# Who subtracts the weights: a hybrid encoder step in which some subtractions and additions go from GpSimd to VectorE

## The chip, the cores and the metric

The kernel runs on one core of a Trainium2 chip. A core has five engines that run side by side, each with its own in-order line of instructions: TensorE (matmuls, "PE" in the profile, its weight loads "PEld"), VectorE ("DVE"), ScalarE ("ACT"), GpSimd ("POOL") and SyncE ("SP"), which here only issues transfers. They meet at semaphores. SBUF is the on-chip memory that they share, PSUM holds the matmul results in banks. The metric is the device time of one execution in microseconds; three executions of the kernel before gave 2524.32, 2525.68 and 2528.39 us, median 2525.68 us.

## The reference, cut to what matters

One layer of a streaming encoder, in float32, for 512 prompt tokens and 8 x 16 sample tokens (640 tokens in all, model width 2048):

```python
xn = rmsnorm(x, norm_mix)
qa, ka, va, qb, kb, vb = split(xn @ w_in)       # 3 x 1024 columns for group A, 1024 + 128 + 128 for group B
oa = band_attend(qa, ka, va, bias)              # 16 heads, own chunk and 8 before
ob = band_attend(rope(qb), rope(kb), vb, sink)  # 16 query heads, 2 key heads, window 128
x = x + concat(rmsnorm(oa), rmsnorm(ob)) @ w_out
h = rmsnorm(x, norm_ffn)
x = x + (silu(h @ w_gate) * (h @ w_up)) @ w_down   # inner width 5632
y = rmsnorm(x, norm_final)
```

The keys and values of both groups are outputs too.

## The kernel before

Everything is held transposed, features on the 128 partitions and the 640 tokens along the free dimension, in two halves of 320. To keep float32 precision with fast matmuls, each operand is split in two parts, `hi` (rounded to the matmul's type) and `lo` (what is left), and each product is three matmuls, `mm3` (L235 to L237): hi by hi, hi by lo, lo by hi. `Net.split` makes the parts: ScalarE writes `hi` (L226), VectorE subtracts it from the source to get `lo` (L227). The third matmul of a set, L237, is the first that needs the weights' `lo`.

The large products are done as **quartets**, a Strassen-like scheme (Winograd's form): four weight blocks b11, b12, b21, b22 against two token halves need seven products p1 to p7 in place of eight. The function `quartet(k, load, lefts, before, after, part, eng)` does one: it loads the four blocks (k chunks of 128 rows by 128 columns each, so k times 128 numbers for a partition), forms the differences of weights, and for each of the seven products splits one block and runs 3 k matmuls. Its differences, in the order of the program:

```python
b12 = b12 - b22        # VectorE, L843
s6  = b11 - b12        # VectorE, L847
p1: split(b11)
b11 = b22 - s6         # on GpSimd here (L850); if eng is VectorE, behind p7 instead (L855)
p6: split(s6);  p7: split(b12)
b21 = b21 - s6         # on eng (L859), behind p2: split(b21)
p5: split(b11);  p4: split(b21);  p3: split(b22)
```

The default of `eng` is `nc.gpsimd`. The order of the products is p1, p6, p7, p2, p5, p4, p3. The four weight tiles are slots of the list "W", the split parts slots of the list "H": four of them, that is two hi-lo pairs, in group A's quartets, six in the feed-forward part. A split therefore waits until TensorE has read the pair two (or three) products back. The products land in PSUM banks ("dn" for p1, p5, p6, p3, two tiles of two banks each; "at" for the others) and VectorE adds them up in SBUF (L869).

The stages, with their place in the profiled span:

- Group B's projections by plain products, to about 277 us.
- **Group A's quartets**, about 270 to 520 us: the loop over `order` runs ten quartets with k = 8, two output tiles each (20 of the 24 tiles of group A's queries, keys and values). After each, `collect` has gathered the two results; VectorE multiplies them by the token norm (L1051) or by it and 1/8 (L1053), and they are stored. During the last quartet the operands of group B's output projection are made (`release`, L231).
- Group A's attention and the sample attention beside the output projections, to about 860 us.
- Gate and up projections by 44 quartets with k = 8, to about 1930 us.
- **The down projection** in 32 steps, `step(t)`, one quartet each over the input blocks `active(t)`: k is 6 in steps 8 to 23 and 5 in the others. The last eight steps, 24 to 31, finish two output tiles each. Behind each of steps 24 to 29, `add_square` squares the two finished tiles on ScalarE (L322) and adds them to the running sum `ssq` (L323), on GpSimd unless told otherwise. Steps 30 and 31 run in an early and a late part, and step 31 alone has `eng=nc.vector`. GpSimd's line also issues the transfers of the activations, `fetch` (L1161).
- The final norm and the stores, from about 2490 us.

The order of instructions on each engine comes from a scheduler that goes by the order of the program, by what its own estimate of time says is ready, and by extra edges that the kernel adds: slots are handed on in order, `keep_follow` holds the first difference (L843) of a step with k under 8 behind the last split before it.

Of the kernel before, what the change touches and what calls it, by code (L numbers as in the profile page):

```python
# [29 lines left out]
STEPS = 32  # L30
# [309 lines left out]
def build(nc, tc, io, pools):  # L340
    n = Net(nc, tc, io, pools)
# [468 lines left out]
    def quartet(k, load, lefts, before=None, after=None, part="all", eng=nc.gpsimd):  # L810

        def product(src, which, bank):
            own = n.get("H"), n.get("H")
            hl = [r(sh(x, k, P)) for x in own]
            at = n.emitted()
            n.split(sh(src, k, P), *hl)
            n.last_split = at, n.emitted()
            if before:
                before(which)
            for j in range(k):  # L820
                n.mm3(bank, (hl[0][:, j], hl[1][:, j]), lefts[j][which][1], j == 0, j == k - 1)
            n.put("H", *own)
            if after:
                after(which)
            return bank

        def get(i):
            t = n.get("W")
            dma(out=sh(t, k, P), in_=load(i))
            return t  # L830

        w = slice(0, k * P)
        sub = ALU.subtract
        if part == "late":
            b21, b22 = get(2), get(3)
            for name, src, which in (("p2", b21, 4), ("p3", b22, 6)):
                yield name, product(src, which, n.bank()[:, :HT])
                n.put("W", src)
            return
        x, y = n.banks(), n.banks()  # L840
        b12, b22, b11 = get(1), get(3), get(0)
        at = n.emitted()
        nc.vector.tensor_tensor(b12[:, w], b12[:, w], b22[:, w], sub)  # L843
        if k < 8:
            n.follow.append((n.last_split, (at, n.emitted())))
        s6 = n.get("W")
        nc.vector.tensor_tensor(s6[:, w], b11[:, w], b12[:, w], sub)  # L847
        yield "p1", product(b11, 0, x[:, 0])
        if eng is nc.gpsimd:
            eng.tensor_tensor(b11[:, w], b22[:, w], s6[:, w], sub)  # L850
        yield "p6", product(s6, 1, y[:, 0])
        yield "p7", product(b12, 2, n.bank()[:, :HT])
        n.put("W", b12)
        if eng is not nc.gpsimd:
            eng.tensor_tensor(b11[:, w], b22[:, w], s6[:, w], sub)  # L855
        b21 = get(2)
        if part == "all":
            yield "p2", product(b21, 4, n.bank()[:, :HT])
        eng.tensor_tensor(b21[:, w], b21[:, w], s6[:, w], sub)  # L859
        n.put("W", s6)  # L860
        yield "p5", product(b11, 3, x[:, 1])
        n.put("W", b11)
        yield "p4", product(b21, 5, n.bank()[:, :HT])
        n.put("W", b21)
        if part == "all":
            yield "p3", product(b22, 6, y[:, 1])
        n.put("W", b22)
# [3 lines left out]
    def collect(steps):  # L871

        y = []
        for name, bank in steps:
            if name == "p1":
                y.append(n.get("S"))
                c11, c21 = y[0][:, :HT], y[0][:, HT:]
                nc.scalar.activation(c11, bank, AF.Identity)
            elif name == "p6":
                y.append(n.get("S"))  # L880
                c12, c22 = y[1][:, :HT], y[1][:, HT:]
                add(c12, c11, bank)
            elif name == "p7":
                add(c21, c12, bank)
            elif name == "p5":
                add(c22, c21, bank)
                add(c12, c12, bank)
            elif name == "p2":
                add(c11, c11, bank)
            elif name == "p4":  # L890
                add(c21, c21, bank)
            elif name == "p3":
                add(c12, c12, bank)
            yield name, y
# [31 lines left out]
    sums = [[None] * 7 for _ in range(8)]  # L926
# [111 lines left out]
    for at in range(0, len(order), 2):  # L1038
        two = order[at:at + 2]
        ws = [io["w_in"][8 * i + p] for i, p in two]  # L1040
        load = lambda z: ws[z % 2][:, 8 * (z // 2):8 * (z // 2) + 8]
        last = at + 2 == len(order)
        if last:
            n.streams = (("heads 0", "heads"), ("decode 0", "decode"), ("heads 1", "heads"), ("decode 1", "decode"))
            for p in range(8):
                heads_of(prompt_a, p, [])
        for _, y in collect(quartet(8, load, sums, split_thirds if at == 0 else None, release if last else None)):
            pass
        for (i, p), x in zip(two, y):
            if i:  # L1050
                nc.vector.tensor_tensor(x, x, r_mix, ALU.mult)  # L1051
            else:
                nc.vector.scalar_tensor_tensor(x, x, 0.125, r_mix, ALU.mult, ALU.mult)  # L1053
            keep_a(i, p, x)
# [13 lines left out]
    r_a, ssq = n.get("S"), n.get("S")  # L1068
# [183 lines left out]
    for i in range(NPAIR):  # L1252
        for src in ("w_gate", "w_up"):
            blocks = [(2 * i, 0), (2 * i + 1, 0), (2 * i, 8), (2 * i + 1, 8)]
            load = lambda z: io[src][blocks[z][0], :, blocks[z][1]:blocks[z][1] + 8]
            y = [n.get("S")]
            c11, c21 = y[0][:, :HT], y[0][:, HT:]
            start, end = i == 0 and src == "w_gate", i == NPAIR - 1 and src == "w_up"
            for step, bank in quartet(8, load, hs, (lambda w: next(prep)) if start else None, free if end else None,
                                      eng=nc.vector if start else nc.gpsimd):  # L1260
# [64 lines left out]
    def step(t, part="all"):  # L1325
        now = active(t)
        nxt = active(t + 1) if t + 1 < STEPS else []
        cnt, q, last = len(now), t % 8, t >= STEPS - 8

        def after(which):  # L1330
            gone = [j for j in now if j not in nxt]
            n.put("S", *(lefts[j][which][0] for j in gone))
            if t == 0:
                fetch_late()
                if which in (0, 1, 2):
                    split_raws()
                    n.follow.append((border, n.later[-1]))
                if which in (2, 4, 3):
                    at = n.emitted()
                    next(final, None)  # L1340
                    n.later.append((at, n.emitted()))
                for x in {3: (0,), 5: (1, 2), 6: (4, 3, 5, 6)}.get(which, ()):
                    keep_last(x)
            waiting.append([(j, which) for j in nxt if j not in now and j != NPAIR - 1])
            fetch_waiting(2)

        if t < 8:
            x, y = n.get("S"), n.get("S")
            sums.append((x, y, n.get("S") if q % 2 == 0 else sums[-1][2]))
            if t == 0:  # L1350
                load_sums()
        x, y, u = sums[q]
        c11, c21, c12, c22 = x[:, :HT], x[:, HT:], y[:, :HT], y[:, HT:]
        us = u[:, HT * (q % 2):HT * (q % 2) + HT]
        o = 2 * sum(len(active(i)) for i in range(q, t, 8))

        def load(z):
            if z == 0 and 0 < t < 8:
                load_sums()
            return io["w_down"][q + 8 * (z % 2), :, o + cnt * (z // 2):o + cnt * (z // 2) + cnt]  # L1360

        for name, bank in quartet(cnt, load, [lefts[j] for j in now], None, after, part,
                                  nc.vector if t == STEPS - 1 else nc.gpsimd):
            if name == "p1":
                if t < 8:
                    nc.scalar.activation(us, bank, AF.Identity)
                else:
                    add(us, us, bank)
                add(c11, c11, bank)
            elif name == "p6":  # L1370
                add(us, us, bank)
            elif name == "p7":
                add(c21, c21, bank)
                add(c22, c22, bank)
            elif name == "p5":
                add(c22, c22, bank)
                add(c12, c12, bank)
            elif name == "p2":
                add(c11, c11, bank)
            elif name == "p4":  # L1380
                add(c21, c21, bank)
            elif name == "p3":
                add(c12, c12, bank)
            if last and name == ("p5" if part == "early" else "p2" if part == "all" else None):
                for c in (c21, c22, c12):
                    add(c, c, us)
            yield name
# [5 lines left out]
    for t in range(STEPS - 2):  # L1393
        run(t)
        if t >= STEPS - 8:
            if t == STEPS - 8:
                ssq = n.get("S")
            for i in range(2):
                n.add_square(ssq, sums[t % 8][i], t == STEPS - 8 and i == 0, "S")
            if t == STEPS - 8:  # L1400
                nc.scalar.activation(n.small(1), ssq[:, :1], AF.Sqrt)

# [141 lines left out]
```

## Time and profile before

| | |
|---|---|
| median of three executions | 2525.68 us |
| profiled execution, its time | 2525.74 us |
| profiled execution, its span | 2523.9 us |
| TensorE busy | 2480.9 us (98%) |
| VectorE busy | 1977.1 us (78%) |
| ScalarE busy | 1055.8 us (42%) |
| GpSimd busy | 697.3 us (28%) |
| GpSimd differences, L850 and L859 | 84 and 84, 182.3 and 186.3 us |
| GpSimd additions of squares, L323 | 29, 49.2 us |

A row of the groups of instructions reads: line, engine, operation, output from inputs, shape, count | busy time, mean ns of one | idle time before them and what ended it. A row of the timeline reads: start in us, length in us, engine, line, operation, and in brackets the idle time before it and what ended that. A row of a table by stage has the stage's bounds, its length, and for each engine its busy time with the number of instructions that ran in it. Matmuls overlap: each is shown some 0.31 us long but the next starts 0.147 us later, so a short pause of TensorE hardly shows in its busy time. The number of matmuls in a stretch shows it better.

### The profile page before, as it was taken

The numbers are of one execution on the slowest core, as the hardware profiler recorded it, in microseconds if no ns is written. First come the engines' busy times: TensorE is split into PE (matmuls) and PEld (weight loads), VectorE is DVE, ScalarE is ACT, GpSimd is POOL, SyncE is SP. The second block draws the span as 40 slices with busy tenths as digits, with TensorE's granted clock in tenths as the row PEclk, the third lists the DMA queues.
The fourth block names the chain that finished last, engine by engine and source line by source line (L and its number), as shares of the span: only waits on it lengthen the run. The fifth ranks groups of instructions, "written<-read, shape, count | busy, mean of one in ns | idle before, by whom it ended". The sixth has DMA issues, their size and how long they took to land.

```text
span 2523.9 us, 44564 instructions
## 1 busy us (share of the span) xinstructions
PE 2480.9 (98%) x17285; PEld 2415.7 (96%) x17285; DVE 1977.1 (78%) x2945; ACT 1055.8 (42%) x1701; POOL 697.3 (28%) x566
## 2 busy tenths in 40 slices
PE   9999999999999999999999999999999999999997
PEld 8888999987899999999999999999999999999997
DVE  7667776685658887788888888888889877777797
ACT  5446333265545543443444343334334333333342
POOL 1001211111002043333323233332325433333353
PEclk9999999999999999999999999999999999999998
DMA  5224433378664334543443344334437766666655
GB/s 198 92 91 122 166 134 124 133 251 289 224 211 155 133 116 146 175 137 122 134 143 128 129 134 144 121 127 143 136 129 260 216 187 181 170 176 177 175 158 182
DMA packets 191604, 401.68 MB, mean 159 GB/s; under 512 B 22496, under 2 KB 83936, under 8 KB 191392
## 3 DMA queue, kind: packets, MB, share of 16 engines
q1 hardware_dynamic: 164608, 340.51, 41.1%
q0 software_dynamic: 23184, 52.77, 7.6%
q10 hardware_dynamic: 3600, 5.55, 0.6%
q8 instruction: 136, 2.23, 0.4%
q14 instruction: 76, 0.62, 0.1%
HBM read 311.14 MB, written 86.87 MB: 158 GB/s over the span
## 4 chain that ended last, share of the span: by engine, by line
PE 87%; DVE 8%; DMA 2%; ACT 1%; issue 1%; POOL 0%; SPq 0%; DVEq 0%; ACTq 0%; POOLq 0%
PE dn L235 17%; PE dn L237 17%; PE dn L236 17%; PE at L237 10%; PE at L236 10%; PE at L235 10%; DVE W L227 2%; PE at L363 2%; PE at L489 1%; DVE S L869 1%; PE at L450 1%; DMA W<-w_in 1%; DMA S<-first_d 1%; ACT W L226 1%; PE at L785 0%
## 5 line engine op out<-in xcount | busy, mean ns | idle before, releaser
L226 ACT ACTIVATE W<-W 128x1024 fp32r<-128x1024 f32 (+2 forms) x662 | 640.3, 968 | 1058.1 <-PE dn L236 559.4
L235 PE MATMUL dn<-S,W 128*128 128x320 f32 x3374 | 1054.3, 313 | 4.2 <-ACT W L226 2.7
L237 PE MATMUL dn<-S,W 128*128 128x320 f32 x3374 | 1045.7, 310 | 7.3 <-DVE W L227 7.0
L236 PE MATMUL dn<-S,W 128*128 128x320 f32 x3374 | 1043.5, 309 | 0.3 <-DVE S L227 0.3
L227 DVE TENSOR_TENSOR W<-W,W 128x1024 fp32r<-128x1024 f32 (+2 forms) x662 | 798.4, 1206 | 93.1 <-ACT W L226 86.0
L235 PEld LDWEIGHTS dn<-S,W 128*128 128x128 f32 x3374 | 633.8, 188 | 19.5 <-issue 14.5
L237 PEld LDWEIGHTS dn<-S,W 128*128 128x128 f32 x3374 | 633.4, 188 | 13.1 <-DVE W L227 11.5
L236 PEld LDWEIGHTS dn<-S,W 128*128 128x128 f32 x3374 | 633.9, 188 | 1.2 <-DVE S L227 0.6
L237 PE MATMUL at<-S,W 128*128 128x320 f32 x1834 | 568.7, 310 | 4.2 <-DVE W L227 4.2
L235 PE MATMUL at<-S,W 128*128 128x320 f32 x1834 | 567.9, 310 | 0.5 <-ACT W L226 0.5
L236 PE MATMUL at<-S,W 128*128 128x320 f32 x1834 | 567.6, 309 | 0.0
L850 POOL TENSOR_TENSOR W<-W,W 128x1024 f32<-128x1024 f32 (+2 forms) x84 | 182.3, 2170 | 776.7 <-DVE W L227 598.2
L237 PEld LDWEIGHTS at<-S,W 128*128 128x128 f32 x1834 | 345.0, 188 | 6.0 <-DVE W L227 5.5
L235 PEld LDWEIGHTS at<-S,W 128*128 128x128 f32 x1834 | 345.1, 188 | 0.8 <-ACT W L226 0.8
L236 PEld LDWEIGHTS at<-S,W 128*128 128x128 f32 x1834 | 345.0, 188 | 0.0
L869 DVE TENSOR_TENSOR S<-S,dn 128x320 f32<-128x320 f32 x398 | 182.0, 480 | 76.0 <-PE dn L237 76.0
L859 POOL TENSOR_TENSOR W<-W,W 128x1024 f32<-128x1024 f32 (+2 forms) x84 | 186.3, 2218 | 185.0 <-DVE W L227 136.8
L869 DVE TENSOR_TENSOR S<-S,at 128x320 f32<-128x320 f32 x292 | 138.1, 482 | 95.6 <-PE at L237 93.5
L843 DVE TENSOR_TENSOR W<-W,W 128x1024 f32<-128x1024 f32 (+2 forms) x86 | 119.5, 1390 | 39.7 <-DMA W<-w_gate 28.1
L847 DVE TENSOR_TENSOR W<-W,W 128x1024 f32<-128x1024 f32 (+2 forms) x86 | 95.8, 1114 | 59.3 <-DMA W<-w_up 33.3
L1161 POOL DMA_DIRECT2D S<-act_d x161 | 87.9, 547 | 160.9 <-PE dn L237 79.6
L1225 DVE TENSOR_TENSOR S<-S,half 128x320 fp32r<-128x320 f32 x147 | 119.7, 835 | 2.9 <-ACT half L1223 1.0
(175 smaller groups left out, 1699.7 us busy)
## 6 DMA issues: line engine op xcount, KB each, us to landing
S<-act_d POOLq DMA_DIRECT2D x161, 320.0 KB, 3.7
W<-w_gate SPq DMA_DIRECT2D x88, 512.0 KB
W<-w_up SPq DMA_DIRECT2D x88, 512.0 KB
W<-w_in SPq DMA_DIRECT2D x66, 512.0 KB
W<-w_down SPq DMA_DIRECT2D x64, 384.0 KB
act_d<-half SPq DMA_DIRECT2D x147, 160.0 KB
act_d<-S SPq DMA_DIRECT2D x147, 160.0 KB
W<-w_down SPq DMA_DIRECT2D x68, 320.0 KB
```

Source lines behind the costliest of these rows:

```text
L226: self.nc.scalar.activation(hi, src, AF.Identity)
L227: self.nc.vector.tensor_tensor(lo, src, f(hi), ALU.subtract)
L235: mm(out, a[0], b[0], start=first, stop=False)
L236: mm(out, a[0], b[1], start=False, stop=False)
L237: mm(out, a[1], b[0], start=False, stop=last)
L843: nc.vector.tensor_tensor(b12[:, w], b12[:, w], b22[:, w], sub)
L847: nc.vector.tensor_tensor(s6[:, w], b11[:, w], b12[:, w], sub)
L850: eng.tensor_tensor(b11[:, w], b22[:, w], s6[:, w], sub)
L859: eng.tensor_tensor(b21[:, w], b21[:, w], s6[:, w], sub)
L869: add = lambda o, a, b: nc.vector.tensor_tensor(o, a, b, ALU.add)
L1161: nc.gpsimd.dma_start(out=r(sh(t, 2, HT)), in_=r(act_d[which, :, j]))
L1225: nc.vector.tensor_tensor(r(src), src, hi, ALU.subtract)
```

## The change

Three places get VectorE where they had GpSimd.

- The ten quartets of group A are called with `eng=nc.vector`. So both differences that GpSimd made there (L850, L859) are VectorE's, and the first of them (then L855) stands behind p7's split in the program, no longer in front of p6's.
- In the down projection `eng` is VectorE for all of the last eight steps, and not for the last alone: seven more steps.
- The additions of squares behind steps 24 to 29 (eleven, since the first square is written straight to `ssq`) go to VectorE; the squares themselves stay on ScalarE.

Nothing that is computed changes.

```diff
@@ group A's loop @@
-        for _, y in collect(quartet(8, load, sums, split_thirds if at == 0 else None, release if last else None)):
+        for _, y in collect(quartet(8, load, sums, split_thirds if at == 0 else None, release if last else None,
+                                    eng=nc.vector)):
             pass
@@ step(t) of the down projection @@
         for name, bank in quartet(cnt, load, [lefts[j] for j in now], None, after, part,
-                                  nc.vector if t == STEPS - 1 else nc.gpsimd):
+                                  nc.vector if t >= STEPS - 8 else nc.gpsimd):
@@ behind steps 24 to 29 @@
             for i in range(2):
-                n.add_square(ssq, sums[t % 8][i], t == STEPS - 8 and i == 0, "S")
+                n.add_square(ssq, sums[t % 8][i], t == STEPS - 8 and i == 0, "S", nc.vector)
```

## The prediction

> **What bounds the kernel now.** I read the busy shares first, then counted matmuls by stage in the stages that the change touches, and then looked in the timeline at what VectorE and GpSimd do at the places where the count falls short.
>
> ```profile
> span 2523.9 us, 44564 instructions
> PE 2480.9 (98%) x17285; PEld 2415.7 (96%) x17285; DVE 1977.1 (78%) x2945; ACT 1055.8 (42%) x1701; POOL 697.3 (28%) x566
> ```
>
> TensorE is the bound: outside its busy time there are 43 us. An edit on another engine can only win back pauses of TensorE in its own stage. Here are the stages (columns: bounds, length, busy time with count for PE, PEld, DVE, ACT, POOL, then clock and transfers):
>
> ```profile
> 1000.00:1900.00 900.00, 900.00 (x6138) 899.91 (x6137) 754.40 (x824) 356.08 (x455) 290.98 (x147) 1.00 0.41 135
> ...
> 270.00:282.00 12.00, 10.51 (x70) 10.02 (x69) 11.00 (x12) 2.77 (x4) 3.35 (x1) 1.00 0.55 187
> 282.00:470.00 188.00, 187.19 (x1268) 185.72 (x1267) 126.74 (x135) 58.51 (x60) 36.19 (x15) 1.00 0.37 129
> 470.00:482.00 12.00, 10.69 (x72) 10.16 (x71) 9.43 (x10) 3.50 (x4) 2.41 (x1) 1.00 0.38 131
> 482.00:510.00 28.00, 28.00 (x193) 28.00 (x192) 16.72 (x20) 10.04 (x11) 4.83 (x2) 1.00 0.48 158
> 510.00:520.00 10.00, 8.29 (x55) 7.77 (x54) 10.00 (x11) 8.14 (x12) 4.10 (x3) 1.00 0.83 278
> 2340.00:2420.00 80.00, 80.00 (x548) 80.00 (x547) 67.34 (x100) 31.75 (x43) 33.47 (x35) 1.00 0.62 176
> 2420.00:2476.00 56.00, 54.33 (x362) 52.89 (x362) 55.81 (x75) 25.38 (x38) 33.31 (x31) 1.00 0.60 171
> 2476.00:2490.00 14.00, 13.22 (x87) 12.42 (x86) 13.65 (x26) 4.92 (x8) 1.66 (x4) 1.00 0.62 189
> 2490.00:2524.00 34.00, 19.54 (x120) 19.01 (x118) 19.27 (x47) 6.55 (x15) 8.37 (x10) 0.70 0.45 155
> ```
>
> The first row is TensorE undisturbed: 900 us / 6136 = 0.1467 us for a matmul (two are always in flight, so each stretch counts two more than start in it). At that rate 12 us holds 84, 188 us 1283.5, 10 us 70, 56 us 384, 14 us 97.5. So TensorE loses 14 matmuls or **2.05 us** at the first quartet of group A, 15.5 or **2.3 us** over its next seven borders, 12 or **1.75 us** at one late border, 15 or **2.2 us** in its last quartet, nothing in between (193 of 193); in the down projection 22 or **3.2 us** from 2420 to 2476 and 10.5 or **1.5 us** to 2490, and nothing before 2420 although VectorE and GpSimd already meet there. That is 13.0 us, the most that this change can win. The last 34 us hold other work and stay.
>
> **What makes VectorE late.** In the last steps VectorE is busy all the time (55.81 of 56 us), yet not by its own work:
>
> ```profile
> 2418.71 2.08 DVE L227 TENSOR_TENSOR W<-W,W 128x640 fp32r<-128x640 f32 x1
> 2420.71 0.47 DVE L869 TENSOR_TENSOR S<-S,dn 128x320 f32<-128x320 f32 x1
> 2421.11 1.80 DVE L227 TENSOR_TENSOR W<-W,W 128x640 fp32r<-128x640 f32 x1
> ...
> 2447.87 0.81 DVE L843 TENSOR_TENSOR W<-W,W 128x640 f32<-128x640 f32 x1
> 2448.61 0.87 DVE L869 TENSOR_TENSOR S<-S,dn 128x320 f32<-128x320 f32 x2
> 2449.40 0.81 DVE L847 TENSOR_TENSOR W<-W,W 128x640 f32<-128x640 f32 x1
> ```
>
> ```profile
> 2418.53 1.57 POOL L850 TENSOR_TENSOR W<-W,W 128x640 f32<-128x640 f32 x1 [2.42 <-DVE W L227]
> 2420.65 1.57 POOL L323 TENSOR_TENSOR S<-S,S 128x640 f32<-128x640 f32 x1
> ```
>
> An operation of the split's size takes 0.81 us at 2447.87 and the split 2.08 or 1.80 us beside a GpSimd operation, while the addition from a PSUM bank (L869, 2420.71) keeps its 0.47 us beside one. So an operation of VectorE with both inputs in SBUF stands still while GpSimd runs one.
>
> The Trainium skill, page "SBUF — State Buffer", section "SBUF: two separate sides", says this of the port pair that the two engines share: it is locked for a whole instruction, the loser fully blocks, and a VectorE operation with at most one SBUF input does not contend. These rows agree, the PSUM addition included: the second split began 0.46 us into the 1.57 us of GpSimd's addition and came out 0.99 us long over, where the lock leaves 1.11. By the lock alone four operations could hold VectorE for 4 x 1.57 = 6.3 us a step and not the 4.4 us that I find below; the last steps would then return all of their 3.2 us, my sum being 2.6.
>
> **The change part by part: the last steps.** From the rows above, consecutive starts give VectorE 0.735 us for a 640-wide operation and 0.40 for a 320-wide addition. A step holds seven splits, two differences and 13 additions: 9 x 0.735 + 13 x 0.40 = 11.8 us. One step lasts 16.2 us and VectorE fills it, so 4.4 us of it is standing still for four GpSimd operations (two differences, two squares), 1.1 us each:
>
> ```profile
> 2418.53:2434.75 16.22, 15.90 (x108) 15.53 (x108) 16.18 (x23) 7.46 (x11) 8.94 (x10) 1.00 0.66 183
> ```
>
> After the change the four cost VectorE 4 x 0.735 = 2.9 us and the 4.4 us go: 14.75 us a step. TensorE needs 105 x 0.1467 = 15.4 us. So VectorE drops below TensorE, by 4%. The pauses end if the scheduler's order fits in that margin; the pairs of slots (three) let the splits run about two products, 4.4 us, ahead. Of the 3.2 us that TensorE loses there I take **2.6** (bounds 0 and 3.2; the case below 0 is a rival). From 2476 GpSimd is nearly idle already (1.66 us), and the 1.5 us there is backlog that VectorE brings along (13.65 of 14 us busy); with less of it about half comes back: **0.8** (0 to 1.5). GpSimd's transfers of activations in the same line come earlier, if anything.
>
> **Group A.** GpSimd's first difference lasts 2.4 us here (2413 ns in the mean of nine) and falls on the border between two quartets, where VectorE has a row of work with both inputs in SBUF:
>
> ```profile
> 347.57 0.83 DVE L1051 TENSOR_TENSOR S<-S,S 128x640 f32<-128x640 f32 x1
> 350.80 1.90 DVE L1051 TENSOR_TENSOR S<-S,S 128x640 f32<-128x640 f32 x1
> ...
> 472.45 1.23 DVE L843 TENSOR_TENSOR W<-W,W 128x1024 f32<-128x1024 f32 x1 [2.25 <-DMA W<-w_in]
> ...
> 476.50 2.73 DVE L1053 SCALAR_TENSOR_TENSOR S<-S,S 128x640 f32<-128x640 f32 x1
> ...
> 510.91 3.83 DVE L231 SCALAR_TENSOR_TENSOR S<-S,gains,S 128x640 fp32r<-128x640 f32 x2
> ```
>
> ```profile
> L1051 DVE TENSOR_TENSOR S<-S,S 128x640 f32<-128x640 f32 x12 | 16.9, 1411 | 0.4
> L1053 DVE SCALAR_TENSOR_TENSOR S<-S,S 128x640 f32<-128x640 f32 x6 | 9.7, 1622 | 0.2
> L850 POOL TENSOR_TENSOR W<-W,W 128x1024 f32<-128x1024 f32 x9 | 21.7, 2413 | 112.9 <-DVE W L227 112.9
> ```
>
> Eighteen of these, two at each of nine borders, cost 26.6 us where 18 x 0.83 = 14.9 would do: 1.3 us of standing still at each border, right ahead of the split of p6, for which L237 then waits. The moved difference costs VectorE 1.13 us (1024 wide, consecutive starts):
>
> ```profile
> 267.60 1.21 DVE L843 TENSOR_TENSOR W<-W,W 128x1024 f32<-128x1024 f32 x1
> 268.73 1.68 DVE L227 TENSOR_TENSOR S<-W,S 128x320 fp32r<-128x320 f32 x4
> ```
>
> If it stands in the same place, 0.2 us is won at each border; if it fits a gap, 1.3. The pauses are mostly 0.3 to 0.6 us, so a little is enough: of 2.3 us I take **1.6** (0 to 2.3). The other difference, L859, is made in the middle of a quartet, beside an idle VectorE:
>
> ```profile
> 332.53 1.06 ACT L226 ACTIVATE W<-W 128x1024 fp32r<-128x1024 f32 x1 [2.41 <-PE dn L236]
> 333.62 1.23 DVE L227 TENSOR_TENSOR W<-W,W 128x1024 fp32r<-128x1024 f32 x1 [0.41 <-ACT W L226]
> 336.19 0.49 DVE L869 TENSOR_TENSOR S<-S,at 128x320 f32<-128x320 f32 x1 [1.35 <-PE at L237]
> ```
>
> There it wins nothing and costs 1.13 us in gaps of 1.35 us; stage-wide VectorE has room (126.74 of 188 us, and 15 x 1.13 = 17 more). What it costs without that cover: a split ends at 334.85 and its third matmul comes at about 336.6 (its slots were free when ScalarE began the same split, 1.09 us ahead of VectorE at 332.53; one product of 24 x 0.1467 = 3.5 us and some matmuls follow), so 1.75 us of slack stands against 1.13. I take 0.
>
> First quartet: L843 took 2.88 us against 1.21 and the reading of a PSUM result queued behind it:
>
> ```profile
> 274.38 2.88 DVE L843 TENSOR_TENSOR W<-W,W 128x1024 f32<-128x1024 f32 x1 [0.48 <-DMA W<-w_in]
> 277.17 0.81 DVE L435 TENSOR_TENSOR S<-dn,S 128x640 f32<-128x640 f32 x1
> ```
>
> 1.67 us go, 1.13 may come in front: 0.54 at least, 2.05 at most, taken **1.2**. Late border: the stretched L1053 (2.73, so 1.9 over) explains the second of two pauses there, about 0.8 us; the first goes back to a late weight load (L843 sat idle 2.25 us for it) and stays. Taken **0.7** (0 to 0.8). Last quartet: the two L231 lose 3.83 - 1.68 = 2.15 us to L859 and would stand behind its 1.13 us instead: **1.0** (0 to 2.2).
>
> **The sum.** 1.2 + 1.6 + 0.7 + 1.0 + 2.6 + 0.8 = 7.9 us. The profiled execution took 2525.74 us (span 2523.9 and 1.8 around it), the median of three is 2525.68; so 2525.7 - 7.9 = **2517.8 us**. The lower ends together give 0.5 us, 2525; the upper ends 12.0, about 2513.7. What a measurement of this kernel can tell from no change is about 0.2%, 5 us, so faster begins below 2520.6.
>
> **The rivals.**
>
> *The stall changes its cause only.* The moved differences stand just where VectorE stood still (0.735 for 1.1, 1.13 for 1.3), in front of the same splits, and a 4% margin is not enough for an in-order line. For it: the program's order makes the difference ready at the same moment as now. Against: each swap is still a small gain. Half of my sum, 4 us: 2521.7, chance 0.27.
>
> *VectorE's line waits for the squares.* An addition of squares now stands in the line that makes every split, and waits there for ScalarE:
>
> ```profile
> 2418.82 0.74 ACT L322 ACTIVATE S<-S 128x640 f32<-128x640 f32 x1 [0.31 <-DVE S L869]
> 2421.22 0.74 ACT L322 ACTIVATE S<-S 128x640 f32<-128x640 f32 x1 [1.03 <-DVE S L869]
> 2407.76 0.74 ACT L226 ACTIVATE W<-W 128x640 fp32r<-128x640 f32 x1 [1.41 <-PE dn L236]
> ```
>
> If nothing is put in between, each costs 0.31 + 0.74 = 1.05 us, and 1.4 more if ScalarE sits on a split that waits for its slots (2407.76). Behind it queue all splits, and TensorE behind those. At 0.3 us a square the margin (15.4 - 14.75) is gone, at 0.73 the step is as long as now (16.2), at 1.1 the gain of group A is used up too (0.8 us a step over five and a half steps). At 1.8 us, between 1.05 and 2.45, a step is 18.35 us: 5.5 x 2.95 = 16.2 lost where 3.2 are now, 13 more, less 4.5 won in group A: 2534, **slower**. Against: VectorE's line has a whole product's work that can stand between a square and its addition. Chance 0.12.
>
> *All comes back,* also the 1.5 us at the end: 2513.7, chance 0.13.
>
> **How the numbers follow.** The forecast, 2515 to 2520.6 with a little above, has 0.48. Faster: 0.13 and 0.43 of the 0.48, 0.56. Same: 0.27 and the 0.05 that is left, with a little of the square case, 0.33. Slower: 0.11. The range takes the upper ends of the terms and part of the square case: 2513 to 2529, with about 0.1 left out on either side.
>
> **What would show it.** The splits of the last steps, today (2385 to 2473):
>
> ```profile
> L227 DVE TENSOR_TENSOR W<-W,W 128x640 fp32r<-128x640 f32 x39 | 49.1, 1259 | 1.3 <-ACT W L226 1.0
> ```
>
> Their mean falls from 1.26 us to 0.82; the step from 16.2 to 15.4 us; VectorE's busy share there from full to about 0.95; L1051 and L1053 to 0.83; 384 matmuls and not 362 in the 56 us before the last two steps. Wrong would be: idle time of VectorE ahead of L323 ended by ScalarE's L322, L237 still waiting for L227 at the borders, or a pause in the gate and up projections that isn't there now.

## The result, and the profile after

The changed kernel took 2513.18 us (median of five, 2512.12 to 2516.12) where the kernel before took 2525.68 us: 12.5 us less, a ratio of 0.9953 with a 95% interval of 0.9942 to 0.9963. That is faster beyond the 0.2% that can be told, inside the range, and 4.6 us below the forecast. It lies only 0.2 us above the range's lower end, 2513. The profiled execution has a span of 2511.4 us:

```profile
span 2511.4 us, 44507 instructions
PE 2474.3 (99%) x17285; PEld 2413.7 (96%) x17285; DVE 1982.9 (79%) x2990; ACT 1055.4 (42%) x1701; POOL 607.1 (24%) x521
```

VectorE took over 45 operations and is busy 6 us more in all; GpSimd is busy 90 us less. The table by stage, on the stretches of the prediction (those of the down projection moved up by the time won before):

```profile
270.00:282.00 12.00, 10.81 (x72) 10.31 (x71) 11.15 (x14) 3.51 (x4) 0.00 (x0) 1.00 0.56 202
282.00:470.00 188.00, 188.00 (x1284) 188.00 (x1283) 136.76 (x152) 59.55 (x61) 0.00 (x0) 1.00 0.38 131
470.00:482.00 12.00, 12.00 (x84) 12.00 (x83) 10.08 (x12) 3.51 (x4) 0.00 (x0) 1.00 0.36 125
...
510.00:520.00 10.00, 9.78 (x67) 9.52 (x66) 9.82 (x14) 8.89 (x13) 2.48 (x5) 1.00 0.83 269
...
2413.00:2469.00 56.00, 56.00 (x384) 56.00 (x383) 54.94 (x96) 26.10 (x39) 8.98 (x17) 1.00 0.69 193
```

1284, 84 and 384 matmuls are the full counts (1268, 72 and 362 before): the pauses over group A's borders and in the last steps are gone. Some 12 matmuls are still missing in the first quartet (14 before), which differs much from one profile to the next, and 3 in the last one (15 before).

The groups of VectorE's instructions, the splits and the additions of squares of the last steps (2375 to 2462) and the multiplications at group A's borders (277 to 512):

```profile
L227 DVE TENSOR_TENSOR W<-W,W 128x640 fp32r<-128x640 f32 x40 | 32.9, 821 | 1.0 <-ACT W L226 0.2
...
L323 DVE TENSOR_TENSOR S<-S,S 128x640 f32<-128x640 f32 x11 | 9.0, 820 | 0.1
...
L1052 DVE TENSOR_TENSOR S<-S,S 128x640 f32<-128x640 f32 x12 | 9.9, 826 | 0.4
L1054 DVE SCALAR_TENSOR_TENSOR S<-S,S 128x640 f32<-128x640 f32 x6 | 5.0, 826 | 0.2
```

The 1259, 1411 and 1622 ns of L227, L1052 and L1054 (then L1051 and L1053) have all become 0.82 to 0.83 us. Nothing stands still any more. And this is where the moved operations went, first at a border of group A, then at a border between two of the last steps:

```profile
347.32 1.22 DVE L227 TENSOR_TENSOR W<-W,W 128x1024 fp32r<-128x1024 f32 x1
348.57 1.22 DVE L855 TENSOR_TENSOR W<-W,W 128x1024 f32<-128x1024 f32 x1
349.71 0.48 DVE L869 TENSOR_TENSOR S<-S,dn 128x320 f32<-128x320 f32 x1
350.23 0.82 DVE L1052 TENSOR_TENSOR S<-S,S 128x640 f32<-128x640 f32 x1
350.97 1.22 DVE L227 TENSOR_TENSOR W<-W,W 128x1024 fp32r<-128x1024 f32 x1
...
2410.82 0.82 DVE L227 TENSOR_TENSOR W<-W,W 128x640 fp32r<-128x640 f32 x1
2411.57 0.82 DVE L855 TENSOR_TENSOR W<-W,W 128x640 f32<-128x640 f32 x1
2412.35 0.49 DVE L869 TENSOR_TENSOR S<-S,dn 128x320 f32<-128x320 f32 x1
2412.76 0.82 DVE L323 TENSOR_TENSOR S<-S,S 128x640 f32<-128x640 f32 x1
2413.49 0.82 DVE L227 TENSOR_TENSOR W<-W,W 128x640 fp32r<-128x640 f32 x1
2414.23 0.82 DVE L323 TENSOR_TENSOR S<-S,S 128x640 f32<-128x640 f32 x1
```

The first difference stands exactly where GpSimd ran it, behind p1's split; in group A part of it falls into a gap of 0.74 us that VectorE had there. The additions of squares follow one another without idle time.

**Where the 12.4 us of the two profiles lie.** TensorE runs the same 17285 matmuls in the same order in all kernels of this text, so for every one its start can be set against its start in the profile of before. The table holds the time won in each stretch (bounds in the time of before), up to the last matmul, for all kernels; the experiments behind it are described below. The last column is for how long the clock stood at half in the 2482 to 2512 stretch, not counting the last spell at half, which begins within 2.5 us of the last matmul and runs to the end in every kernel.

```
                        0-244 244-518 518-1925 1925-2094 2094-2402 2402-2470 2470-2482 2482-2512   half clock
changed kernel           -0.5    6.8     0.0       0.3       0.0       3.0       0.5       2.4       3.4 us
changed kernel again      0.7    6.8     0.0       0.2       0.0       3.0       0.5       0.6       6.8
group A only             -0.4    6.9    -0.9      -0.1       0.0       0.0       0.0       3.2       none
last steps only           0.0   -2.1     0.4      -0.2       0.0       3.0       0.5       2.4       3.4
  squares only            0.5    1.1    -0.3       0.0       0.0      -0.1       0.9       2.5       3.4
  differences only        0.2    0.1     0.1       0.0       0.0       2.5       0.9       2.1       3.4
  first difference only  -0.2   -0.5    -1.7       0.0       0.0       2.8      -1.2       1.6       3.4
group A, first differ.   -0.8    3.9    -0.8      -0.1       0.0       0.0       0.0       1.6       3.4
idle GpSimd reads         0.4    5.9     0.0       0.0      -1.9     -15.6      -5.1       2.4       3.4
idle GpSimd fills         0.1    7.1     0.0      -0.3       0.0       3.0       0.5       0.7       6.8
all quartets              0.2    5.6     0.9       4.4       0.0       3.0       0.5       1.8       3.4
all quartets again        0.7    7.3     0.8       4.3       0.0       3.0      -0.3       2.4       3.4
and the border           -0.8    7.0     0.9       1.4       0.0       3.0       0.4       1.8       3.4
```

The kernel before had 6.8 us of half clock there. Stretches that an edit does not touch differ by up to about 1 us from one execution to the next, and by 2 where the clock drops once more (last steps only, at 280 us; first difference only, at 215 and 519 us; and the border, at 1960 us).

### The profile page after: what moved, and what is told of

It reads as the page before. It is cut to its first block, busy times and chain, and to the rows that moved or that the text cites. A ratio compares the mean times of both kernels' runs of the same rounds, so it can differ in the third digit from the quotient of the medians.

```text
span 2511.4 us, 44507 instructions
## 1 busy us (share of the span) xinstructions
PE 2474.3 (99%) x17285; PEld 2413.7 (96%) x17285; DVE 1982.9 (79%) x2990; ACT 1055.4 (42%) x1701; POOL 607.1 (24%) x521
## 4 chain that ended last, share of the span: by engine, by line
PE 91%; DVE 5%; DMA 2%; ACT 1%; issue 1%; SPq 0%; POOL 0%; DVEq 0%; ACTq 0%; POOLq 0%
PE dn L235 18%; PE dn L237 18%; PE dn L236 18%; PE at L237 10%; PE at L236 10%; PE at L235 10%; PE at L363 2%; PE at L489 1%; DVE W L227 1%; PE at L450 1%; ACT S L463 1%; DVE S L227 0%; PE at L785 0%; DVE S L453 0%; ACT W L226 0%
## 5 line engine op out<-in xcount | busy, mean ns | idle before, releaser
L237 PE MATMUL dn<-S,W 128*128 128x320 f32 x3374 | 1044.0, 310 | 3.8 <-DVE W L227 3.8
L227 DVE TENSOR_TENSOR W<-W,W 128x1024 fp32r<-128x1024 f32 (+2 forms) x662 | 781.1, 1181 | 99.8 <-ACT W L226 91.9
L237 PEld LDWEIGHTS dn<-S,W 128*128 128x128 f32 x3374 | 633.2, 188 | 6.7 <-DVE W L227 5.4
L237 PE MATMUL at<-S,W 128*128 128x320 f32 x1834 | 568.0, 310 | 4.0 <-DVE W L227 4.0
L237 PEld LDWEIGHTS at<-S,W 128*128 128x128 f32 x1834 | 344.9, 188 | 5.3 <-DVE W L227 5.3
L850 POOL TENSOR_TENSOR W<-W,W 128x1024 f32<-128x1024 f32 (+2 forms) x67 | 146.6, 2188 | 629.9 <-DVE W L227 465.3
L869 DVE TENSOR_TENSOR S<-S,dn 128x320 f32<-128x320 f32 x398 | 182.6, 482 | 67.7 <-PE dn L237 66.1
L869 DVE TENSOR_TENSOR S<-S,at 128x320 f32<-128x320 f32 x292 | 138.6, 484 | 85.2 <-PE at L237 82.5
L859 POOL TENSOR_TENSOR W<-W,W 128x1024 f32<-128x1024 f32 (+2 forms) x67 | 150.3, 2244 | 103.6 <-DVE W L227 97.2
```

The lines of the kernel that those rows point to most:

```text
L227: self.nc.vector.tensor_tensor(lo, src, f(hi), ALU.subtract)
L237: mm(out, a[1], b[0], start=False, stop=last)
L869: add = lambda o, a, b: nc.vector.tensor_tensor(o, a, b, ALU.add)
```

## The experiments

Theory: an operation of VectorE with two inputs in SBUF stands still while a GpSimd operation that reads SBUF runs, and TensorE's pauses come from that. Rival: GpSimd's results come late for who reads them, since it takes twice as long for the same work.

**Each place alone.** First group A alone:

```diff
-        for _, y in collect(quartet(8, load, sums, split_thirds if at == 0 else None, release if last else None)):
+        for _, y in collect(quartet(8, load, sums, split_thirds if at == 0 else None, release if last else None,
+                                    eng=nc.vector)):
```

> Group A's two differences on VectorE, the last eight steps as before. If VectorE's operations with two inputs in SBUF stand still beside a GpSimd operation (the theory), group A's pauses go as they do with the whole change: TensorE is about 6 us ahead by 530 us and stays so, the last steps keep their 362 matmuls in 56 us, and the time is about 2519.5 us. If the gain of group A and that of the steps are not additive (a later wait takes the first one back), it ends above 2522.

2517.16 us, ratio 0.9965 (0.9953 to 0.9978). TensorE wins 6.9 us in group A, nothing in the last steps. The stage's gain is kept to the end. The time is 2.3 us below what I had said; the profile has 3.2 us more in the last 30 us, which this edit does not touch. Then the last steps alone:

```diff
-                                  nc.vector if t == STEPS - 1 else nc.gpsimd):
+                                  nc.vector if t >= STEPS - 8 else nc.gpsimd):
...
-                n.add_square(ssq, sums[t % 8][i], t == STEPS - 8 and i == 0, "S")
+                n.add_square(ssq, sums[t % 8][i], t == STEPS - 8 and i == 0, "S", nc.vector)
```

> The differences of steps 24 to 30 and the eleven additions of squares on VectorE, group A as before. Theory: VectorE's step falls from 16.2 to 15.4 us (TensorE's own time), 3.2 us come back before step 30 and 1.5 in steps 30 and 31, and if the tail's 1.5 us go with that: 2519.5 us; if the tail's part of the gain was the clock of one execution and not this edit, 2521.

2520.81 us, ratio 0.9981 (0.9972 to 0.9990). All 3.0 us of the steps are back, and 0.5 behind them, as in the whole change. So the two places add up, and neither needs the other.

**The last steps taken apart.** The squares alone are the second of those two hunks, the differences alone the first.

> Only the eleven additions of squares on VectorE. Nobody reads the running sum before the final norm. If VectorE stands still beside GpSimd (theory), two of four stalls of 1.1 us a step go and 2 x 0.735 us come: 16.2 - 2.2 + 1.5 = 15.5 us a step against TensorE's 15.4, so 2.5 to 4 us are won: about 2522.5. If GpSimd's results are late for their readers (rival), nothing changes or VectorE's added work makes it worse: 2525.7 to 2530.

> Only the differences of steps 24 to 30 on VectorE, squares on GpSimd. Theory: the same arithmetic as for the squares alone, 15.5 us a step, about 2522.5. Rival (late results): the differences are the only ones with a reader, so all of what the steps can win: about 2519.5 to 2521, clearly more than the squares alone.

The squares alone: 2523.41 us, ratio 0.9991 (0.9982 to 1.0000), and nothing won from 2402 to 2470. The differences alone: 2522.04 us, 0.9980 (0.9971 to 0.9989), 2.5 us won there and 0.9 behind. My arithmetic by load gave both the same 15.5 us a step, and that is refuted: same load, 0.8 us against 3.4, both stretches together. It looks like the rival's result, but the timeline of the kernel with the squares alone shows another reason:

```profile
2431.24 0.82 DVE L227 TENSOR_TENSOR W<-W,W 128x640 fp32r<-128x640 f32 x1
2431.98 0.48 DVE L869 TENSOR_TENSOR S<-S,at 128x320 f32<-128x320 f32 x1
2432.38 2.07 DVE L227 TENSOR_TENSOR W<-W,W 128x640 fp32r<-128x640 f32 x1
2434.37 0.81 DVE L323 TENSOR_TENSOR S<-S,S 128x640 f32<-128x640 f32 x1
2435.11 0.47 DVE L869 TENSOR_TENSOR S<-S,dn 128x320 f32<-128x320 f32 x1
```

and its waits of TensorE (engine, line, waited for: us in total, times, longest):

```profile
PE dn L235 <- DVE S L869: 2.3, 3, 1.6
```

TensorE waits for no result of GpSimd here; ScalarE does, before the split of b21 (4.9 us in all), but TensorE's waits name no such split. TensorE waits for p3's PSUM bank of the step before, which L869 at 2435.11 reads out; ahead of that in VectorE's line stand a split stretched to 2.07 us by the first difference on GpSimd, and now an addition of squares as well. Taking the squares from GpSimd put 0.74 us in front of the one instruction that TensorE was waiting for.

So one operation of the four should matter most, the first difference. It alone in the last steps:

```diff
-        eng.tensor_tensor(b21[:, w], b21[:, w], s6[:, w], sub)
+        (nc.gpsimd if k == 5 and not n.both else eng).tensor_tensor(b21[:, w], b21[:, w], s6[:, w], sub)
```

(with the first hunk of the steps; `n.both` is set ahead of step 31.)

> The kernel before, with the first difference alone (L850, then L855) of steps 24 to 30 on VectorE; the second and the squares stay on GpSimd. The theory by VectorE's whole load of a step gives a step of 11.8 + 3 x 1.1 + 0.74 = 15.8 us, still over TensorE's 15.4, so TensorE would gain at most half of the 3 us from 2402 to 2470. The theory by place (only what stands still ahead of the reading of p3's bank at the border between two steps makes TensorE pause, all else is taken up by the slots' lead) gives 2.5 to 3 us of the 3, from this one operation of four.

2522.6 us, ratio 0.9984 (0.9974 to 0.9994). One operation of four wins 2.8 of the 3.0 us up to 2470, as the place would have it. But 1.2 us of it is given back right behind, so 1.6 us are left. There two more splits, at 2472 and 2474 us, are stretched to 1.92 and 1.82 us beside the two additions of squares that stayed on GpSimd, and L237 waits for VectorE's splits (1.5 us). A late weight load, for which GpSimd's difference waited 3.7 us, may have its part. So place decides which standing still reaches TensorE; that what is left of it then uses up the lead of the three pairs of slots fits this one profile and was not tested alone.

**GpSimd work that nobody reads.** This tells standing still from late results. The changed kernel, with an idle subtraction on GpSimd behind each moved operation of steps 24 to 30, into a tile `d` that nothing reads:

```diff
+    def beside(x):
+        if own:
+            d = own[0]
+            nc.gpsimd.tensor_tensor(d, d, x, ALU.subtract)
```

> The changed kernel with idle work added: behind each of the moved operations of steps 24 to 30 GpSimd subtracts the same 640 numbers a partition from a tile that nobody reads (four a step, like those that were moved away). No result of the kernel waits for it. Theory (standing still): VectorE needs 14.75 + 4 x 1.1 = 19.1 us a step against 15.4, six to seven steps: 15 to 22 us slower than the changed kernel, 2528 to 2535. Rival (late results, or GpSimd's line): no more than 1 us, 2513 to 2514.

2540.59 us (two executions), ratio 1.0062 (1.0044 to 1.0081). The last steps lose 15.6 us against the kernel before, 18.6 against the changed one, and 5.1 more behind; some 1.7 us of that are the clock, which stood at half for 3.4 us there. From 2385 to 2473 VectorE's splits are stretched again, the additions of squares most of all (the first two rows; the third is the idle subtraction):

```profile
L227 DVE TENSOR_TENSOR W<-W,W 128x640 fp32r<-128x640 f32 x30 | 35.5, 1183 | 3.3 <-ACT W L226 3.3
L323 DVE TENSOR_TENSOR S<-S,S 128x640 f32<-128x640 f32 x9 | 17.1, 1903 | 0.0
...
L816 POOL TENSOR_TENSOR S<-S,S 128x640 f32<-128x640 f32 x9 | 21.0, 2333 | 23.5 <-DVE S L879 23.2
```

No result is late, and some 27 us are lost against the changed kernel: standing still is enough. TensorE waits for the stretched splits there (2402 to 2470):

```profile
PE at L237 <- DVE W L227: 8.3, 8, 1.2
PE dn L237 <- DVE W L227: 3.6, 3, 1.2
```

One instruction does wait for the idle work: ScalarE's L1438, which scales in place a finished tile that the idle subtraction reads (7.4 us from 2385 to 2473). But VectorE, busy for 84.6 of these 88 us, stood idle ahead of its splits for 3.3 us only, so this can be a small part at most. (I had said 2528 to 2535; the two engines hold up each other, GpSimd's 1.57 us having become 2.33.) The same with fills, which only write SBUF:

```diff
+            nc.gpsimd.tensor_tensor(d[:, :1], d[:, :1], x[:, :1], ALU.subtract)
+            nc.gpsimd.memset(d, 0.0)
+            nc.gpsimd.memset(d, 0.0)
```

> As the kernel with idle subtractions on GpSimd, but each is one number wide and followed by two fills of 640 numbers, which write SBUF and read none of it. If VectorE stands still for any GpSimd operation that uses SBUF, it stands still for about as long as before: 10 us slower than the changed kernel or more. If only reading GpSimd operations block it (the Trainium skill, SBUF — State Buffer, SBUF: two separate sides, says so), within 1 us of the changed kernel: 2513 to 2514.

```profile
L227 DVE TENSOR_TENSOR W<-W,W 128x640 fp32r<-128x640 f32 x39 | 32.0, 820 | 0.7
...
L818 POOL MEMSET S<- 128x640 f32 x22 | 14.0, 638 | 0.9
L817 POOL MEMSET S<- 128x640 f32 x21 | 13.3, 634 | 1.2
```

2514.58 us, ratio 0.9960 (0.9947 to 0.9973), where the changed kernel had 0.9953; all 3.0 us of the steps are kept. GpSimd is busy for 43 us of these 68 (2402 to 2470), more than the 38 in the kernel with the reads, and VectorE's splits stay at 0.82 us. GpSimd was busy for 39 of the same 68 us in the kernel before; so a freer line of GpSimd, with its transfers issued earlier, is not what the change wins either. So the rule of the Trainium skill, page "SBUF — State Buffer", section "Who interferes with whom", that a VectorE operation with two SBUF inputs contends with a GpSimd instruction that reads SBUF and not with one that only writes it, holds here. (What the prediction takes from that page, that an operation with at most one SBUF input does not contend, the page states with a condition that the prediction left out: outside the 2-port perf modes.)

**Group A's two differences.** The first on VectorE, the second left on GpSimd:

```diff
-        eng.tensor_tensor(b21[:, w], b21[:, w], s6[:, w], sub)
+        second = nc.gpsimd if k == 8 and lefts is sums else eng
+        second.tensor_tensor(b21[:, w], b21[:, w], s6[:, w], sub)
```

> Group A's first difference (the one on the border) on VectorE, the second on GpSimd, the steps as before. Theory: the 1.3 us of standing still at each border go, so the pauses of 0.3 to 0.6 us over the seven borders go (2.3 us); the pause at the late border and that of the last quartet, where the second difference runs beside L231, stay at least in part: TensorE 3 to 4 us ahead by 530 us, time about 2522. Rival: the second difference is what counts, since its slot is what the next weight load waits for: less than 1 us.

2521.95 us, ratio 0.9990 (0.9981 to 0.9999); 3.9 us won in group A, of 6.8. The borders are quiet, the last quartet is as before:

```profile
282.00:470.00 188.00, 188.00 (x1282) 187.70 (x1281) 126.24 (x142) 59.33 (x61) 19.31 (x8) 1.00 0.38 130
470.00:482.00 12.00, 11.38 (x78) 10.98 (x76) 10.28 (x12) 3.72 (x5) 0.00 (x0) 1.00 0.39 135
510.00:520.00 10.00, 8.29 (x55) 7.76 (x54) 10.00 (x13) 8.12 (x11) 2.15 (x3) 1.00 0.83 261
```

The 55 matmuls from 510 to 520 are those of the kernel before: there the second difference runs beside L231. The late border gets half of its matmuls back (78, between 72 and 84). The profile of before has a possible reason, in the waits of the queue that issues the weight loads:

```profile
SPq L829 <- POOL W L859: 17.1, 2, 8.6
```

A weight load waits there for the second difference, whose source is the slot that it needs. On VectorE that difference ends at 458.3 us where GpSimd ended it at 462.2; some 2.5 us of that is the lead that TensorE has by then, so it is over a microsecond earlier. That the load came earlier for this reason was not tested alone, and this border proves little: in the kernels with the squares alone and with the differences alone, where group A is untouched, it was 1.3 and 1.0 us better by itself. What the second difference is worth is shown by the last quartet, where L231 still takes 3.84 us beside it.

**All quartets.** The differences of the gate and up quartets and of steps 0 to 23 on VectorE too (`eng` is `nc.vector` everywhere):

> The changed kernel with the differences of all other quartets on VectorE too (gate and up, steps 0 to 23). In 1000 to 1900 us TensorE has no pause to win back (6138 matmuls in 900 us), so by the theory no change there, although VectorE's work falls in part: 2512 to 2514. Slower, by some us, if VectorE's line gets too full where it also makes the products' parts: 2516 to 2525.

2509.16 us, ratio 0.9937 (0.9924 to 0.9949). Run again beside the changed kernel on one chip:

> The kernel with every quartet's differences on VectorE once more, on one chip with the changed kernel. From the first pair of profiles: 4 us below the changed kernel, all of it at the border from the gate and up projections to the down projection (1930 to 1970 us), none in the 900 us from 1000 to 1900.

> The changed kernel once more, as the other side of that comparison: 11 to 13 us below the kernel before, TensorE 6 to 7 us ahead at 575 us, 3 us more between 2402 and 2470; the gain of the last 30 us between 0 and 3 us, by how long the clock stands at half there (6.8 us, 3.4 us or not at all).

2507.49 us, 0.9927 (0.9913 to 0.9940; 2525.82 us for the kernel before), against 2512.97 us, 0.9946 (0.9933 to 0.9958), for the changed kernel: 5.5 us faster than the change, 18 faster than before. First the kernel with all quartets, then the changed kernel on that chip:

```profile
1000.00:1900.00 900.00, 900.00 (x6139) 900.00 (x6138) 722.19 (x899) 362.70 (x461) 115.53 (x74) 1.00 0.42 136
1925.00:1970.00 45.00, 42.21 (x283) 41.16 (x282) 42.57 (x69) 20.96 (x38) 20.81 (x28) 1.00 0.96 320
```

```profile
1000.00:1900.00 900.00, 900.00 (x6138) 899.90 (x6137) 756.59 (x824) 358.29 (x460) 292.54 (x147) 1.00 0.41 135
1925.00:1970.00 45.00, 39.34 (x255) 37.04 (x254) 43.11 (x60) 19.98 (x39) 30.55 (x37) 1.00 1.00 330
```

In the 900 us nothing is won, since TensorE has no pause there, although VectorE does 75 operations more and is busy 34 us less. The gain lies where I had not looked, at the border to the down projection, which still had pauses: 4.3 us. What GpSimd has left at that border, moved as well:

```diff
-                (nc.vector, nc.gpsimd)[a].tensor_tensor(lo, part, f(hi), ALU.subtract)
+                nc.vector.tensor_tensor(lo, part, f(hi), ALU.subtract)
...
-        (nc.vector, nc.gpsimd)[which % 2].tensor_tensor(lo, kept.pop(which), f(hi), ALU.subtract)
+        nc.vector.tensor_tensor(lo, kept.pop(which), f(hi), ALU.subtract)
...
-        tt = nc.gpsimd.tensor_tensor
+        tt = (nc.vector if i == NPAIR - 1 else nc.gpsimd).tensor_tensor
```

> Every quartet's differences on VectorE, and the ten subtractions of parts and two of sums that GpSimd still makes at that border. TensorE still loses 3.8 us there. If those go with GpSimd's operations: up to 2 us less than with the quartets alone, since 12 x 0.4 us come to VectorE's line; if that line is what is full there: no change, within 1 us.

2508.61 us, 0.9933 (0.9921 to 0.9946): nothing more to win, 1.4 us at the border where the quartets alone win 4.3. Of the 2.9 us between them some 1.7 are the clock, which stood at half for 3.4 us there in the profiled execution; whether the rest is VectorE's line stays open.

## Why the prediction was right, and where it was off

*What bounds the kernel.* Right: what the edit wins lies in TensorE's pauses, and where there were none nothing changed (2094 to 2402: 0.0 in all kernels without idle work).

*Standing still.* Right, and the two idle-work kernels show it directly: with reads the time is some 27 us above the changed kernel's, with fills 1.4 us, and the kernel before alone differs by 1.7 us between the chips.

*The sum.* The forecast was too careful in group A: 1.2 + 1.6 + 0.7 + 1.0 = 4.5 us, measured 6.8. Of its four terms the borders were mis-sized (1.6 for a pause of 2.3 that went entirely), the late border (0.7 of 1.75; all of it went, where I had put half down to a late weight load that would stay), and the last quartet (1.0 of 2.2; three matmuls, 0.4 us, are left). The first quartet gave 2 matmuls, 0.3 us, of 1.2, but one profile can't judge this term: in the eight kernels with the same edit of group A it gave 0.0 to 1.5 us, 1.3 in the second profile of the changed kernel. The borders gave 2.3 us and the last quartet 1.75 in all eight; the late border gave 0.7 to 1.8, and up to 1.3 in kernels that leave group A alone, so that its share is not sure. The second difference, which I put at 0 but for the last quartet, is what the last quartet needed: without it none of the 1.75 us comes. (By counts the four come to 6.2 us; the other 0.6 of the 6.8 this execution made good between 244 and 262 us, ahead of the stage.)

*The last steps.* 2.6 and 0.8 us against 3.0 and 0.5: right in size, in part by luck. The reasoning by VectorE's load was only half of it. It gave the same answer for the squares as for the differences; the squares alone won nothing in those steps. What fails in it is the step "four GpSimd operations, 1.1 us each", as if each counted alike. VectorE's share was forecast at 0.95 and is 0.98 (54.94 of 56), likely because rows overlap by 0.08 us, which the forecast by starts leaves out.

*The last 34 us, put at 0.* Not so in the profiles, and not the change either. The same 166 matmuls from 2482.4 us on in four kernels, before, changed, changed again, and group A alone:

```profile
2482.40:2512.40 30.00, 26.64 (x166) 25.88 (x165) 21.45 (x49) 8.83 (x17) 4.23 (x5) 0.85 0.34 112
```

```profile
2472.50:2502.50 30.00, 24.50 (x166) 24.01 (x164) 22.29 (x52) 9.16 (x18) 5.66 (x7) 0.91 0.38 125
```

```profile
2471.40:2501.40 30.00, 26.29 (x165) 25.75 (x164) 20.80 (x47) 9.01 (x18) 4.21 (x5) 0.84 0.37 121
```

```profile
2477.10:2507.10 30.00, 23.23 (x166) 22.47 (x164) 24.05 (x56) 9.16 (x18) 6.49 (x8) 0.95 0.41 136
```

The granted clock in this stretch was 0.85, 0.91, 0.84 and 0.95, with 6.8, 3.4, 6.8 and 0 us at half speed (the last spell again not counted), and the stretch came out 0, 2.4, 0.6 and 3.2 us shorter. The same changed kernel has both values, so it is no part of the change. That leaves 6.8 + 3.0 + 0.5 = 10.3 us by the profiles for a difference of 12.5 us between medians (12.9 on the other chip). Where the other 2 us are is open in part. The medians of several variants, the squares alone too (2.8 us), lie some 2 us further below the kernel before than their edited stretches explain, but not of all: the differences alone 0.8 us, and group A's first difference alone lies 1.3 us the other way. The granted clock of every execution, which is on record to 0.001, is 0.9960 in the mean of 57 executions of the kernel before and 0.9964 in that of ten of the changed kernel; over 2520 us that is about 1 us, some of which may fall behind the last matmul, where it costs less. The rest was not found.

*The rivals.* "The stall changes its cause only" had the fact right, the moved difference stands just where GpSimd's stood, and the consequence wrong, except for the squares alone. "VectorE's line waits for the squares" did not come about: VectorE had 0.1 us of idle time ahead of all eleven additions. "All comes back" gave 2513.7, and the time is there, but by another sum: 10.3 of the 13.0 us of pauses came back. In this the forecast had luck too. The pauses that came back give 2515.4 us, inside the range; the 2 us below that, which bring the time to the range's very end, are not of the sum.

## What to carry to other kernels

A busy engine may be busy standing still: compare the length of one and the same instruction with and without a neighbour's operation before believing a busy share. Work of GpSimd that reads SBUF was not free here beside a VectorE line that feeds the matmuls; moved to VectorE an operation 640 wide cost 0.74 us where it had held VectorE for 1.1 in the mean, and GpSimd work that only writes cost nothing that could be told. What it is worth still depends on place: look for what stands in VectorE's line ahead of the split or the bank read for which TensorE waits, and move that first, and only in stages where TensorE pauses.

## What was unexpected of the hardware

In these profiles TensorE's clock fell to half behind pauses of 1.2 to 1.9 us, for 3.4 or 6.8 us, and not in every execution: the pause of 1.93 us at about 2496 us is in every kernel, and in the one with group A only the clock stayed full behind it. In the last 30 us that moved up to 3.2 us, as much as the last steps themselves. The kernel with the last steps only met it at group A's first quartet, which its edit doesn't touch; the stage from 262 to 282 us there, with a clock of 0.96:

```profile
262.00:282.00 20.00, 17.89 (x115) 17.39 (x114) 18.40 (x24) 8.73 (x17) 6.05 (x3) 0.96 0.70 240
```

At 276.3 us TensorE started nothing for 1.9 us and then once for 0.8; at 280.2 the clock fell for 3.4 us, and the stretch to 518 us came out 2.1 us longer than before. But for the one that runs to the end of the program, the half-speed stretches of all profiles last 3.4 us or twice that. The Trainium skill, page "TensorE: Matmul & The Clock Gate", section "What's actually happening", gives a free-running window of 3413 ns, which agrees; that the clock falls after an idle window of that length, as it also says, doesn't: no pause in front of these drops was as long, 1.9 us being the longest.
